# Scratch of q and k laid out by head and then feature, q and k loaded as 128 plain rows, and V's quarters in the order 0, 2, 1, 3, in a one-core decoder block

## The chip, the cores and the metric

The kernel runs on one core of a Trainium2 chip. Its engines are TensorE (PE in the profile, with its weight loads as PEld), VectorE (DVE), ScalarE (ACT), GpSimd (POOL) and SyncE (SP), which here does nothing but issue DMAs, in the order in which they stand in its queue. The data of all DMA queues is moved by 16 DMA engines. The metric is the device time of one execution in microseconds, as the median of several runs.

## The reference, cut to what matters

One layer of a decoder block on x of 2048 positions by 1024 features, all float32:

- `proj = x @ W_in + b_in`, with 9216 output columns: q, k and v for 3 groups of 8 heads of 64 features, two SiLU gates, the input of a gated linear recurrence, and two merge gates.
- Rotary embedding on q and k. Then dilated causal attention: group g has window and dilation (128, 1), (512, 4), (2048, 16). Queries and keys of one group are gathered by their residue modulo the dilation, and 128 queries attend to the keys of their own block of 128 and, in groups 0 and 1, of the block before.
- The three groups' outputs are combined per head slot, weighted by their softmax denominators, times a SiLU gate, and projected.
- A second branch: a causal convolution of width 4, the recurrence over positions, a SiLU gate, a projection.
- `out = (sigmoid(gA) * yA + sigmoid(gB) * yB) @ W_out + b_out`, and a layer norm of `alpha * x + out`.

## The kernel before, in words

Three stages follow one another on TensorE.

**Stage A, the projection (about 6 to 1437 us).** Features lie on the 128 partitions, positions in four chunks (c) of 512. Each pass of the plan takes two blocks of 128 output features through a Strassen-like scheme of products (line 639). Each factor is split in a high and a low part, so that three products stand for one in float32. q and k blocks hold two heads of 64 features: the weights' columns are permuted so that feature d of head h sits on partition 2d + h (`by_head`, line 274). After the rotation (`qk_chain`, line 320) a tile of 128 partitions by 512 positions (256 KB) is stored to a scratch in HBM, `qk_scr["q" or "k", u]`, one scratch of 128 rows by 2048 positions for each block u = 4g + hp of group g and head pair hp. q of group 2 and k of group 1 are stored grouped by residue (lines 350 and 353; runs of 32 and 128 positions), the others as plain rows of 512 positions (line 356). There are 96 such stores, 16 + 16 + 64.

**Stage B, attention (about 1437 to 1790 us).** It goes through 12 units u of one head pair of one group each (`unit(u)`: groups 0, 2, 1 for each head pair in turn), four steps G to a unit, 48 steps in all. Step G holds the scores of two blocks pairs (lines 994 and 1000, out of tile `qk`), their masking and exponential (DVE, ACT), the turning of the weights (line 1031), the values (line 1064, out of tile `V`), and, from G = 4 on, a half of a job of the other branch's projection (`yb`, line 1234). Tiles `qk` and `V` are double buffered by u % 2. q of unit u + 1 is loaded at the end of step 4u, k at 4u + 1 (`qk_parts`, line 794), V at 4u + 1 and 4u + 2 in four quarters of 32 partitions (`v_parts`, line 808). Since the scratch has the two heads in turn in its rows, q and k each are loaded in two halves: rows 0, 2, 4, ... to partitions 0 to 63, rows 1, 3, 5, ... to partitions 64 to 127 (line 803). Each half is 64 rows of 8 KB.

Every three units (one head pair done) the running maxima and sums go through HBM to be laid out anew: turned and stored (`ml_scr`, line 1088), loaded (`mt`, lines 1097, 1101, 1104), worked on in three steps by DVE, ACT and POOL (`weights`, line 1107), stored by POOL (`w_scr`, line 1145) and loaded as `wh` (line 1151). A matmul spreads them over the partitions (`w`, line 1158), and the three groups' outputs are weighted with them.

**Stage C (about 1790 us to the end)** holds what is left of `yb`, the attention branch's projection (`ya`) and the last product with the layer norm (`z`).

The order on every engine is the order in which the program's text runs. SP's queue carries nearly all loads and stores of stage B: q, k, V, `wlr` (weights of `yb`), `hx` (its input), `gB`, `yb_scr`, `ml_scr`, `mt`, `wh`, `ga`. The table `todo` (`at_group`) tells after which step an issue stands. In the built program each DMA that SP issues also waits until the one issued eight places before it has landed, since eight completion counters are used in turn.

Of the kernel before, what the change touches and what calls it, by code (L numbers as in the profile page):

```python
# [15 lines left out]
P = 128  # L16
# [4 lines left out]
CH = 512  # L21
# [10 lines left out]
def hybrid_block_kernel(ctx: ExitStack, tc: tile.TileContext, a: dict, out: bass.AP):  # L32
    nc = tc.nc
    sp, act, dve, pool, pe = nc.sync, nc.scalar, nc.vector, nc.gpsimd, nc.tensor

    def flat(t):
        return t.bitcast(F32)
# [14 lines left out]
    qk_scr = {(n, u): dram.tile([P, S], F32, name=f"{n}_scr{u}") for u in range(12) for n in ("q", "k")}  # L52
# [53 lines left out]
    def big(slot, shape, dt, name):  # L106
        return (cur["Z"] if slot[0] == "Z" else X).tile(shape, dt, name=name, tag=slot)
# [44 lines left out]
    def take(name, dt=F32R):  # L152
        if not vacant:
            raise RuntimeError(f"no slot at {now['n']}: {[x[1].name if hasattr(x[1],'name') else x[1] for x in home.values()]} chains {len(chains)}")
        i = vacant.pop(0 if now["n"] < now["last"] else vacant.index(min(vacant, key=LAST_SLOTS.index)))
        t = sl_p.tile([P, CH], dt, tag=f"s{i}", name=name)
        home[id(t)] = (i, t)
        return t

    def give(*ts):  # L160
        for t in ts:
            vacant.append(home.pop(id(t))[0])

    def give_sent(*ts):

        for t in ts:
            later(2, lambda t=t: give(t))
# [71 lines left out]
    def tt(eng, out, in0, in1, op):  # L239
        eng.tensor_tensor(out=out, in0=in0, in1=in1, op=op)  # L240
# [70 lines left out]
    lo_, up_ = slice(0, 64), slice(64, P)  # L311
# [4 lines left out]
    def blocks(t, g):  # L316

        return t.rearrange("p (r j) -> p j r", r=4 if g == 1 else 16)

    def qk_chain(rw, f, c):  # L320
        isq = f < FT_K
        u = f % 12
        g = u // 4
        nm = f"{f}_{c}"
        yield Ask(lag=0, need=1, ACT=1.3)
        sw = take("sw" + nm)
        scale = 0.125 if isq else 1.0
        act.activation(flat(sw)[lo_], flat(rw)[up_], AF.Copy, scale=scale)  # L328
        act.activation(flat(sw)[up_], flat(rw)[lo_], AF.Copy, scale=scale)  # L329
        yield Ask(lag=1, DVE=1.5 if c < 2 else 1.0, POOL=1.7)  # L330
        cos, sin = CS[c % 2]
        if isq:
            dve.scalar_tensor_tensor(out=flat(rw), in0=flat(rw), scalar=0.125, in1=cos, op0=ALU.mult, op1=ALU.mult)
        else:
            tt(dve, flat(rw), flat(rw), cos, ALU.mult)
        tt(pool, flat(sw), flat(sw), sin, ALU.mult)
        yield Ask(lag=1, need=1 if g else 0, DVE=(1.45 if c < 2 else 1.2) if g else 1.0)
        if g == 0:
            rp = rw
            tt(dve, flat(rp), flat(rw), flat(sw), ALU.add)  # L340
            give(sw)
        else:
            rp = take("rp" + nm)
            v, r = "p (j r) -> p j r", 4 if g == 1 else 16
            tt(dve, blocks(flat(rp), g), flat(rw).rearrange(v, r=r), flat(sw).rearrange(v, r=r), ALU.add)
            give(rw, sw)
        yield Ask()
        dst = qk_scr["q" if isq else "k", u]
        if isq and g == 2:
            sp.dma_start(dst.rearrange("p (r i) -> p r i", r=16)[:, :, 32 * c:32 * c + 32],  # L350
                         flat(rp).rearrange("p (r i) -> p r i", r=16))
        elif g == 1 and not isq:
            sp.dma_start(dst.rearrange("p (r i) -> p r i", r=4)[:, :, P * c:P * c + P],
                         flat(rp).rearrange("p (r i) -> p r i", r=4))
        else:
            sp.dma_start(dst[:, c * CH:(c + 1) * CH], flat(rp))
        give_sent(rp)


# [197 lines left out]
    qk = [("qk", FT_K + u, FT_Q + u) for u in range(12)]  # L557
# [26 lines left out]
    def result(s, fi, c, bank, u):  # L584
# [10 lines left out]
        if kind in ("qk", "v"):  # L595
            y = take("y" + nm)
            if kind == "v" and fi:
                dve.scalar_tensor_tensor(out=flat(y), in0=u, scalar=b72[:, f:f + 1], in1=bank, op0=ALU.add, op1=ALU.subtract)
            else:
                total(flat(y), bank, u, f, sgn, True)  # L600
            start_chain(qk_chain(y, f, c) if kind == "qk" else v_chain(y, f, c))
        elif kind == "mg":
            y = take("y" + nm, F32)
            total(y, bank, u, f, sgn, False)
            start_chain(mg_chain(y, sgn, f, c))
        elif kind == "ga" or not fi:
            y = take("y" + nm, F32)
            total(y, bank, u, f, sgn, False)
            start_chain(silu_chain(y, sgn, f, c))
        else:  # L610
            i = f - FT_U
            if c == 1 and i in put_off:
                y = take("y" + nm, F32)
                total(y, bank, u, f, sgn, True)
                act.activation(ubs[:, i, 2, 0:3], y[:, CH - 3:CH], AF.Copy)
                start_chain(store_chain(y, u_scr[i]))
                return
            ub = ub_free.pop(0)
            total(ub[:, 3:3 + CH], bank, u, f, sgn, True)
            start_chain(lru(i, c, ub), 7 if c % 2 else 0)  # L620
# [95 lines left out]
    for s, pl in enumerate(plan):  # L716
        if pl[0] and pl[4] == "ug":
            i = pl[1][1][0] - FT_U
# [68 lines left out]
    AT_X = {}  # L787
    UG = {0: 0, 2: 1, 1: 2}

    def unit(u):  # L790

        return (0, 2, 1)[u % 3], u // 3

    def qk_parts(u):

        g, hp = unit(u)

        def part(x, h, hs):
            def fn():
                if u < 2 and (x, h) == (0, 0):  # L800
                    AT_X["qk", u] = big(("X2", "X3")[u], [P, 2, S], F32, f"qk{u}")
                src = qk_scr["qk"[x], 4 * g + hp].rearrange("(d h) s -> h d s", h=2)
                sp.dma_start(AT_X["qk", u % 2][hs, x], src[h])
            return fn

        return [part(x, h, hs) for x in range(2) for h, hs in ((0, lo_), (1, up_))]

    def v_parts(u):
        g, hp = unit(u)
        src = v_scr[g][hp]  # L810

        def part(q):
            def fn():
                if u == 0 and q == 0:
                    AT_X["v"] = big("X4", [P, 2, 2, 16, 64], F32, "V")
                v = AT_X["v"][32 * q:32 * q + 32, u % 2]
                if g == 2:
                    sp.dma_start(v.rearrange("i s n x -> i (s n) x"), src[q].rearrange("s (a i) x -> i (s a) x", a=4))
                else:
                    for t in range(2):  # L820
                        sp.dma_start(v[:, t], src[t, q].rearrange("c (a i) x -> i (c a) x", a=4))
            return fn

        return [part(i) for i in range(4)]


    def biases():
# [45 lines left out]
    for t in sorted(early):  # L873
        for fn in early[t]:
            at(max(t, 0), fn)

    begin = {1: qk_parts(0), 3: v_parts(0), 5: qk_parts(1)}
    low = NS
    where = [(s, j) for s in range(NQ) for j in range(ticks[s])]
# [18 lines left out]
    n = len(where)  # L898
# [383 lines left out]
    def at_group(g, fn):  # L1282
        todo.setdefault(g, []).append(fn)
# [14 lines left out]
    for fn in v_parts(1):  # L1298
        at_group(1, fn)
# [6 lines left out]
        at_group((1, 1, 2, 2, 3, 3, 4, 4)[k], lambda k=k: split_h(k))  # L1306
    for u in range(1, 11):
        for i, fn in enumerate(qk_parts(u + 1)):
            at_group(4 * u + i // 2, fn)
        for i, fn in enumerate(v_parts(u + 1)):  # L1310
            at_group(4 * u + 1 + i // 2, fn)
    WS = {}
# [19 lines left out]
    for hp in range(3):  # L1332
        e = 4 * (3 * hp + 2) + 4
        for i in range(12):
            c, g = i // 3, (0, 2, 1)[i % 3]
# [3 lines left out]
    for G in range(NG + 1):  # L1339
# [30 lines left out]
        if y:  # L1370
            n, hf = divmod(halves[0], 2)
# [82 lines left out]
    for t in halves:  # L1454
        n, hf = divmod(t, 2)
# [139 lines left out]
    for t, tt in enumerate(TT):  # L1595
        c, b = divmod(t, 4)
# [67 lines left out]
```

## Time and profile before

| What | us |
|---|---|
| median of 3 runs (2122.76 to 2126.47) | 2124.85 |
| profiled execution, its time | 2128.92 |
| profiled execution, span from first to last instruction | 2127.1 |
| TensorE busy in the span | 2078.8 (98%) |
| VectorE, ScalarE, GpSimd busy | 1683.5, 1189.1, 763.6 |
| TensorE busy between 1420 and 1790 us | 343.57 of 370 |
| mean share of the 16 DMA engines between 1420 and 1790 us | 0.95 |

The profiled execution lies 4.07 us above the median of the runs; 1.8 us of its time lie outside the span. "DMA share" in a window is the busy time of the packets summed over the 16 engines, over 16 times the window; it can pass 1, since an engine may hold two packets at once. "PEclk" is the clock granted to TensorE as a share of the full one. The duration of an entry of SPq is the time that SP took to issue the DMAs, not the time of the transfer.

### The profile page before, as it was taken

The page shows a single profiled execution, that of the slowest core. Times are in us where ns is not written, and L with a number is a line of the kernel's source. Part 1 is how long each engine was busy: PE and PEld are TensorE (multiplying, and loading weights), DVE is VectorE, ACT ScalarE, POOL GpSimd, SP SyncE. Part 2 cuts the span into 40 slices and gives each one's busy share as a digit, 9 for nine tenths or more (in the row PEclk, how much of TensorE's full clock was granted, in tenths as well). Part 3 has the DMA queues.
Part 4 walks back from the last instruction along what each step waited for, and adds up shares of the span by engine and source line. Part 5 has one row for each costly group of instructions (what it writes and reads, how often), then busy time and mean ns, then how long its engine had stood idle before and what let it go on. Part 6 is the DMA issues. An engine that isn't in the chain of part 4 may idle for free. (4 is left out here: it accounts for less than half of the span.)

```text
span 2127.1 us, 35284 instructions
## 1 busy us (share of the span) xinstructions
PE 2078.8 (98%) x11877; PEld 1695.7 (80%) x11877; DVE 1683.5 (79%) x2985; ACT 1189.1 (56%) x2462; POOL 763.6 (36%) x685
## 2 busy tenths in 40 slices
PE   9999999999999999999999999998999889999998
PEld 7888888877788888888887888887877678778886
DVE  8788999988988868888887888756666567877667
ACT  6456455557467566677577777756666554321100
POOL 2544654553664200120120120116267478522120
PEclk9999999999999999999999999999999999999999
DMA  7877887976887866666665666679999996774431
GB/s 229 243 230 206 246 248 210 271 231 189 250 252 218 274 204 198 183 199 191 212 193 178 217 208 201 194 214 234 197 234 214 204 209 195 240 239 151 156 99 70
DMA packets 333445, 443.09 MB, mean 208 GB/s; under 512 B 164320, under 2 KB 174592, under 8 KB 330192
## 3 DMA queue, kind: packets, MB, share of 16 engines
q1 hardware_dynamic: 316624, 408.38, 65.0%
q0 software_dynamic: 11744, 23.54, 6.0%
q10 hardware_dynamic: 4896, 8.92, 1.1%
q8 instruction: 94, 1.54, 0.3%
q14 instruction: 87, 0.71, 0.1%
HBM read 289.74 MB, written 150.99 MB: 207 GB/s over the span
## 5 line engine op out<-in xcount | busy, mean ns | idle before, releaser
L639 PE MATMUL q<-xT,hS 128*128 128x512 f32 x1632 | 503.7, 390 | 0.0
L639 PE MATMUL q<-xT,l 128*128 128x512 f32 x1088 | 423.8, 390 | 3.0 <-DVE l L240 2.9
L639 PE MATMUL q<-xB,hA 128*128 128x512 f32 x1344 | 415.5, 390 | 0.3 <-ACT hA L284 0.3
L639 PE MATMUL q<-xB,l 128*128 128x512 f32 x944 | 367.2, 389 | 0.0
L639 PEld LDWEIGHTS q<-xT,hS 128*128 128x128 f32 x1632 | 305.5, 188 | 66.7 <-issue 3.3
L639 PEld LDWEIGHTS q<-xB,hA 128*128 128x128 f32 x1344 | 251.4, 188 | 56.8 <-issue 4.1
L639 PEld LDWEIGHTS q<-xT,l 128*128 128x128 f32 x1088 | 204.3, 188 | 47.5 <-DVE l L240 5.1
L240 POOL TENSOR_TENSOR sw<-sw,sin 128x512 f32<-128x512 f32 x96 | 155.4, 1624 | 157.9 <-ACT sw L329 85.9
L639 PEld LDWEIGHTS q<-xB,l 128*128 128x128 f32 x944 | 177.2, 188 | 36.8
L240 POOL TENSOR_TENSOR y<-y,h 128x512 f32<-128x512 f32 x28 | 39.1, 1398 | 385.3 <-DVE h L538 340.2
L1016 ACT ACTIVATE pb<-pb 128x192 f32<-128x192 f32 (+1 forms) x384 | 160.6, 421 | 30.1 <-DVE pb L1014 28.5
L639 PE MATMUL q<-xB,hS 128*128 128x512 f32 x544 | 167.7, 389 | 1.0 <-ACT hS L284 1.0
L639 PE MATMUL q<-xT,hA 128*128 128x512 f32 x544 | 168.0, 390 | 0.2 <-ACT hA L284 0.2
L284 ACT ACTIVATE hS<-S 128x512 fp32r<-128x512 f32 x170 | 108.3, 637 | 84.8 <-DVE S L240 69.6
L1234 PE MATMUL yb<-hx,wl 128*128 128x512 f32 x576 | 150.3, 402 | 1.9 <-POOL hx L1210 1.7
L284 ACT ACTIVATE hA<-wA 128x512 fp32r<-128x512 f32 x220 | 138.2, 635 | 21.1 <-DMA wA<-in_w_in_dram 5.5
L240 POOL TENSOR_TENSOR l<-wA,hA 128x512 fp32r<-128x512 f32 x68 | 107.7, 1584 | 77.3 <-ACT hA L284 45.5
L1234 PEld LDWEIGHTS yb<-hx,wl 128*128 128x128 f32 x576 | 104.9, 188 | 31.4 <-issue 6.8
L639 PEld LDWEIGHTS q<-xB,hS 128*128 128x128 f32 x544 | 102.0, 188 | 22.8 <-ACT hS L284 1.4
L639 PEld LDWEIGHTS q<-xT,hA 128*128 128x128 f32 x544 | 101.8, 188 | 22.6 <-issue 1.1
L328 ACT ACTIVATE sw<-y 64x512 f32<-64x512 f32 x96 | 60.6, 631 | 79.2 <-DVE y L580 71.8
L1510 POOL TENSOR_TENSOR me<-gA,me 128x512 f32<-128x512 f32 x30 | 47.7, 1604 | 159.3 <-DVE gA L1509 136.1
(215 smaller groups left out, 4340.1 us busy)
## 6 DMA issues: line engine op xcount, KB each, us to landing
wA<-in_w_in_dram SPq DMA_DIRECT2D x220, 256.0 KB
wl_scr<-l SPq DMA_DIRECT2D x102, 512.0 KB
l<-wl_scr SPq DMA_DIRECT2D x102, 512.0 KB
wS<-in_w_in_dram SPq DMA_DIRECT2D x102, 256.0 KB
wS<-in_w_in_dram POOLq DMA_DIRECT2D x68, 256.0 KB, 6.6
wlr<-in_w_f_dram SPq DMA_DIRECT2D x64, 256.0 KB
mg_scr<-y SPq DMA_DIRECT2D x59, 256.0 KB
v_scr<-vs SPq DMA_DIRECT2D x48, 256.0 KB
```

What stands on the lines that cost most here:

```text
L240: eng.tensor_tensor(out=out, in0=in0, in1=in1, op=op)
L284: act.activation(heads(h), heads(r, False), AF.Copy)
L328: act.activation(flat(sw)[lo_], flat(rw)[up_], AF.Copy, scale=scale)
L639: pe.matmul(bank, w[:, ks], x[:, kk, xx], start=(first and i == 0), stop=(last and i == 11))
L1016: act.activation(pp, pp, AF.Exp, scale=-1.0, bias=mm, accum_out=ll)
L1234: pe.matmul(YB["t"], w[:, a, k], hx(8 * c + k)[:, b], start=(hf == 0 and m == 0), stop=(hf == 1 and m == 11))
L1510: (dve if i in (6, 7) else pool).tensor_tensor(out=ME[c][:, f], in0=ga, in1=ME[c][:, f], op=ALU.add)
```

## The change

The scratch of q and k has the heads one after the other: row 64h + d instead of 2d + h. The tile in SBUF that is stored stays as it is (feature d of head h on partition 2d + h). So a plain store now writes each partition's row of 2 KB to row 64h + d, as one DMA whose HBM side has the shape 64 x 2 x 512. The two stores grouped by residue are each cut in two DMAs, one for a head, which read every second partition. A load of q or of k is then one DMA of 128 rows of 8 KB instead of two of 64 rows; part 0 (q) stays at step 4u, part 1 (k) at 4u + 1. V's quarters are loaded in the order 0, 2 (at 4u + 1), 1, 3 (at 4u + 2), instead of 0, 1 and 2, 3.

```diff
@@ qk_chain @@
         dst = qk_scr["q" if isq else "k", u]
-        if isq and g == 2:
-            sp.dma_start(dst.rearrange("p (r i) -> p r i", r=16)[:, :, 32 * c:32 * c + 32],
-                         flat(rp).rearrange("p (r i) -> p r i", r=16))
-        elif g == 1 and not isq:
-            sp.dma_start(dst.rearrange("p (r i) -> p r i", r=4)[:, :, P * c:P * c + P],
-                         flat(rp).rearrange("p (r i) -> p r i", r=4))
-        else:
-            sp.dma_start(dst[:, c * CH:(c + 1) * CH], flat(rp))
+        if g == 2 - (not isq):
+            r = 16 if isq else 4
+            n = CH // r
+            for h in range(2):
+                sp.dma_start(dst[64 * h:64 * h + 64].rearrange("d (r i) -> d r i", r=r)[:, :, n * c:n * c + n],
+                             flat(rp).rearrange("(d h) (r i) -> h d r i", h=2, r=r)[h])
+        else:
+            sp.dma_start(dst.rearrange("(h d) s -> d h s", h=2)[:, :, c * CH:(c + 1) * CH], flat(rp))
         give_sent(rp)
@@ qk_parts @@
-        def part(x, h, hs):
+        def part(x):
             def fn():
-                if u < 2 and (x, h) == (0, 0):
+                if u < 2 and x == 0:
                     AT_X["qk", u] = big(("X2", "X3")[u], [P, 2, S], F32, f"qk{u}")
-                src = qk_scr["qk"[x], 4 * g + hp].rearrange("(d h) s -> h d s", h=2)
-                sp.dma_start(AT_X["qk", u % 2][hs, x], src[h])
+                sp.dma_start(AT_X["qk", u % 2][:, x], qk_scr["qk"[x], 4 * g + hp])
             return fn
-        return [part(x, h, hs) for x in range(2) for h, hs in ((0, lo_), (1, up_))]
+        return [part(x) for x in range(2)]
@@ v_parts @@
-                if u == 0 and q == 0:
+                if u == 0 and not q:
...
-        return [part(i) for i in range(4)]
+        return [part(i) for i in (0, 2, 1, 3)]
@@ the table of steps @@
         for i, fn in enumerate(qk_parts(u + 1)):
-            at_group(4 * u + i // 2, fn)
+            at_group(4 * u + i, fn)
```

On SP, in stage A, around one of the stores grouped by residue. Before (`wl_scr` keeps low parts of weights, `rp` is a rotated tile, `wS` and `wA` are weights):

```order
L247 DMA wA_4_891<-in_w_in_dram 128x512
L350 DMA q_scr_106<-rp_1_865 2048x1x32
L301 DMA wl_scr_117<-l_3_835 128x1024
L356 DMA k_scr_107<-rp_0_918 128x512
L301 DMA wl_scr_117<-l_3_887 128x1024
L247 DMA wS_5_986<-in_w_in_dram 128x512
```

and of the change:

```order
L247 DMA wA_4_891<-in_w_in_dram 128x512
L353 DMA q_scr_106<-rp_1_865 1024x1x32 x2
L301 DMA wl_scr_117<-l_3_835 128x1024
L356 DMA k_scr_107<-rp_0_919 64x2x512
L301 DMA wl_scr_117<-l_3_887 128x1024
L247 DMA wS_5_987<-in_w_in_dram 128x512
```

One grouped store has become two in the same place, and the plain store has another shape; no other row of stage A stands elsewhere.

On SP, in stage B, from the load of q for unit 8 to the loads of `wh` for the second head pair. Before:

```order
L803 DMA qk_13619<-q_scr_102 64x2048 x2
L1218 DMA gB_16928<-mg_scr 128x512
L1245 DMA yb_scr<-gB_16680 128x512
L1088 DMA ml_scr_64<-mls_16926 64x128
L803 DMA qk_13619<-k_scr_103 64x2048 x2
L821 DMA V<-v_scr_84 32x16x64 x4
L1184 DMA wlr_17024<-in_w_f_dram 128x512
L821 DMA V<-v_scr_84 32x16x64 x4
L1151 DMA wh_13747<-w_scr_71 12x512
```

and of the change:

```order
L802 DMA qk_13651<-q_scr_102 128x2048
L1217 DMA gB_16943<-mg_scr 128x512
L1244 DMA yb_scr<-gB_16696 128x512
L1087 DMA ml_scr_64<-mls_16941 64x128
L802 DMA qk_13651<-k_scr_103 128x2048
L820 DMA V<-v_scr_84 32x16x64 x4
L1183 DMA wlr_17038<-in_w_f_dram 128x512
L820 DMA V<-v_scr_84 32x16x64 x4
L1150 DMA wh_13775<-w_scr_71 12x512
```

The q and k rows are one DMA each instead of two, in the same places; the eight V issues read alike, though the second two of the first four now go to partitions 64 to 95. TensorE, VectorE, ScalarE and GpSimd have the same instructions in the same order as before.

## The prediction

> **What bounds the kernel now.** I read first, in windows, whether TensorE stands anywhere, and how full the DMA engines are there (busy time of each engine, with its count of instructions, then TensorE's clock, DMA share and rate):
>
> ```profile
> core 0: us, PE busy (x) PEld busy (x) DVE busy (x) ACT busy (x) POOL busy (x), PEclk, DMA share, GB/s
> 1300.00:1420.00 120.00, 120.00 (x534) 97.82 (x533) 90.86 (x128) 88.67 (x138) 18.22 (x12) 1.00 0.65 206
> 1420.00:1790.00 370.00, 343.57 (x4231) 277.51 (x4230) 233.84 (x994) 224.56 (x911) 215.49 (x263) 0.98 0.95 212
> ```
>
> The end of stage A is TensorE alone: 120.00 busy of 120. Around stage B, TensorE stands 370 - 343.57 = 26.4 us, its clock is not full, and the DMA engines are 0.95 full while they move only 212 GB/s. So a change to stage B's transfers can win some 26 us and what the clock loses, no more. What TensorE waited for there:
>
> ```profile
> PE w L1158 <- DMA wh<-w_scr: 12.3, 3, 8.1
> PE pt L1031 <- ACT ptb L1044: 5.4, 3, 4.4
> PE pt L1031 <- ACT pb L1016: 2.2, 2, 2.1
> PE yb L1234 <- POOL hx L1210: 1.7, 3, 0.7
> ```
>
> Never for q, k or V themselves, which are loaded a unit ahead. It waits for `wh`, a load of 24 KB. TensorE's order of time at its four longest stops (start, duration, last the idle time before it):
>
> ```profile
> 1568.43 0.47 PE L1158 MATMUL w<-wh,sel 128*128 128x512 f32 x1 [1.54 <-DMA wh<-w_scr]
> ...
> 1662.88 0.76 PE L1158 MATMUL w<-wh,sel 128*128 128x512 f32 x1 [8.09 <-DMA wh<-w_scr]
> ...
> 1729.38 0.72 PE L1031 MATMUL pt<-ident,pb 64*128 64x64 f32 x16 [4.36 <-ACT ptb L1044]
> ...
> 1755.06 0.47 PE L1158 MATMUL w<-wh,sel 128*128 128x512 f32 x1 [2.62 <-DMA wh<-w_scr]
> ```
>
> Why `wh` is late stands in SP's order of time ahead of the longest stop, beside what the same issues take when nothing holds them (minimum/median/maximum in ns), and the median from issue to landing of `w_scr`, from which `wh` is loaded:
>
> ```profile
> 1633.75 0.88 SPq L1184 DMA_DIRECT2D wlr<-in_w_f_dram  x2
> 1634.73 1.14 SPq L803 DMA_DIRECT2D qk<-q_scr  x2
> 1635.92 0.58 SPq L1218 DMA_DIRECT2D gB<-mg_scr  x1
> 1639.00 0.33 SPq L1245 DMA_DIRECT2D yb_scr<-gB  x1
> 1639.43 0.47 SPq L1088 DMA_DIRECT2D ml_scr<-mls  x1
> 1639.95 1.23 SPq L803 DMA_DIRECT2D qk<-k_scr  x2
> 1642.47 5.55 SPq L821 DMA_DIRECT2D V<-v_scr  x4
> 1648.19 4.71 SPq L1184 DMA_DIRECT2D wlr<-in_w_f_dram  x2
> 1652.95 2.58 SPq L821 DMA_DIRECT2D V<-v_scr  x4
> 1656.01 4.23 SPq L1151 DMA_DIRECT2D wh<-w_scr  x4
> ```
>
> ```profile
> L821 SPq DMA_DIRECT2D V<-v_scr x64: 303/488/3979, 1427.1 to 1748.6; - x64
> L1151 SPq DMA_DIRECT2D wh<-w_scr x16: 333/362/3007, 1563.1 to 1824.2; - x16
> ```
>
> ```profile
> w_scr<-whl POOLq DMA_DIRECT2D x8, 48.0 KB, 7.3
> ```
>
> Four V issues take 5.55 us instead of 4 x 0.488 = 1.95, two `wlr` 4.71 instead of 0.88, four V 2.58, four `wh` 4.23 instead of 4 x 0.362 = 1.45. Together SP loses 3.60 + 3.83 + 0.63 + 2.78 = 10.8 us between 1642 and 1660, held by transfers that are not through. The 8.09 us stop is this backlog, and the first transfers in it are q's and k's halves.
>
> **The rate of those halves.** Three windows in which one kind of transfer prevails: loads of weights and x over 128 rows at the start, q and k of unit 0 in halves, V's quarters.
>
> ```profile
> 10.00:20.00 10.00, 10.00 (x45) 8.27 (x45) 9.34 (x18) 9.71 (x18) 0.00 (x0) 1.00 1.04 386
> 1427.00:1433.00 6.00, 6.00 (x28) 4.99 (x27) 1.82 (x3) 0.63 (x1) 0.00 (x0) 1.00 1.01 215
> 1633.00:1635.00 2.00, 2.00 (x44) 1.93 (x40) 1.48 (x9) 2.00 (x10) 1.79 (x4) 1.00 1.39 159
> ```
>
> At an equally full DMA (1.04 and 1.01), loads over 128 partitions bring 386 GB/s, those over 64 bring 215. Row length can't be the cause: the halves have the longer rows (8 KB against 2 KB). So I take it that a transfer over half of the partitions has about half of the way into SBUF.
>
> **The change part by part.**
>
> *q and k as one DMA of 128 rows.* A unit's q and k are 2 x 128 x 8 KB = 2.10 MB: 9.75 us at 215 GB/s, 5.43 at 386. The new load itself is in no row. Lower bound of its worth: 0, if the rate stays; upper: 4.3 us a unit, 52 us of queue time over twelve units, which brings the share from 0.95 to about 0.95 - 52/370 = 0.81. I take the upper, since the nearest row is of the same partitions. SP also issues 24 DMAs fewer.
>
> Longest stop: if only 4.3 us of the 10.8 go, `wh` comes 4.3 earlier and 8.09 - 4.3 = 3.8 remain. But SP stands until 1639.00 for `yb_scr` whatever the DMA does; q (2.7 us at the new rate) is then through, and k, issued at 1639.95, is through by about 1643, just as V's issue begins at 1642.47. So V and `wlr` find free engines, and the whole 10.8 us can go. Next late is `w_scr`, which POOL issues here:
>
> ```profile
> 1642.74 1.09 POOL L1145 DMA_DIRECT2D w_scr<-whl  x2 [0.30 <-POOL whl L240]
> ```
>
> Its end at 1643.83 and 7.3 to landing give 1651.1; 1.45 for the `wh` issues and the 2.64 that lie today between their end (1660.24) and TensorE's start give 1655.2, against 1654.79 when TensorE stops. Residue 0.4; gain **7.7 us** (between 4.3 and 8.09).
>
> The two shorter `wh` stops, 1.54 and 2.62, are below 4.3 and have the same issues ahead: gain **4.2 us** (between 0 and 4.2).
>
> The clock around the long stop:
>
> ```profile
> 1656.00:1663.00 7.00, 0.12 (x1) 0.15 (x1) 0.00 (x0) 0.00 (x0) 3.68 (x4) 0.66 0.85 103
> 1663.00:1667.00 4.00, 4.00 (x28) 3.16 (x30) 1.47 (x5) 0.41 (x2) 0.00 (x0) 0.50 0.81 224
> 1667.00:1671.00 4.00, 4.00 (x36) 3.40 (x35) 2.49 (x15) 3.70 (x18) 0.00 (x0) 0.81 1.03 223
> 1730.00:1735.00 5.00, 5.00 (x42) 4.52 (x39) 2.81 (x11) 2.88 (x14) 1.01 (x2) 0.66 1.07 282
> 1740.00:1790.00 50.00, 47.38 (x569) 38.26 (x568) 34.05 (x133) 30.31 (x125) 36.44 (x38) 1.00 0.70 175
> ```
>
> After 8.09 us of standing, TensorE works at 0.50 and 0.81: 4 x 0.50 + 4 x 0.19 = 2.8 us lost. After 4.36 us it loses 5 x 0.34 = 1.7; after 2.62 us (within 1740 to 1790) nothing. Gain with the long stop gone: **2.8 us**.
>
> The 4.36 us stop is ACT standing 6.42 us for `mt`, whose preparation stands on POOL behind splits of `hx`; POOL itself waited for a DMA only here:
>
> ```profile
> 1711.63 0.62 POOL L1209 CAST hx<-hx 128x512 fp32r<-128x512 f32 x1 [1.11 <-DMA hx<-hb_scr]
> 1728.33 0.52 ACT L1131 ACTIVATE mt<-mt 32x384 f32<-32x384 f32 x1 [6.42 <-DMA V<-v_scr]
> ```
>
> So an earlier DMA gives 1.1 at most of it; I take **0.9** (between 0 and 4.36 + 1.7).
>
> *V's quarters 0, 2, 1, 3.* Quarters 0 and 1 in a row run at 159 GB/s, so a unit's 1.05 MB take 6.6 us. If 0 and 2 ran side by side, each on its own half, it would be 3.3: worth 0 to 3.3 us of queue time a unit. No row shows two quarters of different halves in flight. I take 0, since they stand one after the other in one queue; and more would change little, the stops it could shorten being counted as gone. [...]
>
> *The stores.* Stage A gets 32 more DMAs. The grouped stores' issues:
>
> ```profile
> L350 SPq DMA_DIRECT2D q_scr<-rp x16: 519/564/967, 69.6 to 1271.0; - x16
> L353 SPq DMA_DIRECT2D k_scr<-rp x16: 518/542/577, 462.1 to 1407.7; - x16
> ```
>
> Each half of such a store takes between half of that and all, so SP has 32 x 0.28 to 0.56, 9 to 18 us, more in 1340. The 64 plain stores (64 x 2 x 512) might fall to the lower rate: 262 KB take 0.68 us at 386 and 1.22 at 215, so 64 x 0.54 = 35 us more of queue time. The cover is the DMA share of 0.65 and TensorE's 120.00 of 120: weights come ahead of time. I take 0; without the cover, up to 18 + 35 = 53 us.
>
> **Sum:** 7.7 + 4.2 + 2.8 + 0.9 = 15.6 us, against the profiled execution 2128.92 - 15.6 = 2113.3. That execution lies 4.07 us above the median of the runs. If none of the 4.07 lies in these stops, the median falls to 2124.85 - 15.6 = 2109.3; if all does, to 2113.3. I take the middle: **2111 us**.
>
> **Rivals.**
>
> *Half of the long stop stays.* V's slow quarters hold SP even without q and k, or POOL's chain to `w_scr` becomes the last. For it: V moves but 159 GB/s and stands nearest ahead of `wh`; `w_scr` has a margin of only 0.4 us. Against: SP's pause until 1639.00. Then 4.3 of the long stop and 4.2 of the short ones go, the clock still falls (3.8 lies nearer to 4.36, where it fell, than to 2.62): 8.5 us, 2116. [...]
>
> *The change doesn't do what it says: the rate stays at 215.* For it: no row has 8 KB rows over 128 partitions, and 212 GB/s is what the whole stage moves. Against: 386 in the first row at the same share. Then nothing goes: 2125.
>
> *Slower: the stores hold back stage A.* Place: SP's queue, where weights (`wA`, `wS`, `l`) stand behind the stores; price up to the 53 us above, less 15.6: 2162. It decides once each of the 96 stores costs TensorE over (15.6 + 4.2)/96 = 0.21 us. Against it: TensorE never waits for a DMA in the row of 1300 to 1420.
>
> **How the numbers follow.** Forecast 0.60, half stays 0.18, rate stays 0.14, slower 0.08. Low end: all of the waits quoted for TensorE (21.6) and both clock losses (4.5) but what ACT's own chain keeps, some 4: 2124.85 - 22, about 2103. High end: 2122, past the second case; what lies above is the two last, 0.22 together. 0.2% (4.2 us) is about what a measurement of this kernel tells from no change. Faster by more: 0.78; within: 0.14; slower: 0.08.
>
> **What would show it.** Right: in stage B a DMA share of some 0.8, q and k of unit 0 at over 330 GB/s, V and `wlr` issues near their medians at the second head pair, no stop of `w` for `wh` over 1 us, the clock at 1.00 from 1650 to 1670. Wrong: a share near 0.95 (rate stays); `w` still waiting over 3 us with SP held at V or at `w_scr` (half stays); new idle time at line 639 (stores).

## The result, and the profile after

The changed kernel takes 2104.37 us in the median (2102.49 to 2105.95, 4 runs), the kernel before beside it 2125.66 (4 runs). The ratio is **0.9893, 95% interval 0.9862 to 0.9923**: 22.7 us less (16.4 to 29.3). Forecast were 2111 us, a gain of 15.6 us by the sum and 13.9 in the stated time. The profiled execution took 2103.79 us against 2128.92, 25.1 us less; its span is 2102.0.

The same windows as before, of the kernel after. Stage B now ends about 26 us earlier, so the second row ends at 1770 (columns as in the prediction's windows):

```profile
core 0: us, PE busy (x) PEld busy (x) DVE busy (x) ACT busy (x) POOL busy (x), PEclk, DMA share, GB/s
1300.00:1420.00 120.00, 120.00 (x535) 97.86 (x534) 90.38 (x128) 89.15 (x139) 18.24 (x12) 1.00 0.65 206
1420.00:1770.00 350.00, 344.13 (x4261) 279.58 (x4260) 238.01 (x1000) 226.20 (x914) 220.79 (x267) 1.00 0.84 229
1427.00:1431.00 4.00, 4.00 (x19) 3.31 (x18) 1.07 (x2) 0.61 (x1) 0.55 (x1) 1.00 0.97 373
1650.00:1670.00 20.00, 20.00 (x248) 15.77 (x247) 15.70 (x55) 13.27 (x55) 12.00 (x11) 1.00 0.94 251
```

TensorE stands 350 - 344.13 = 5.87 us around stage B, where it stood 26.4. q and k of unit 0 as 128 rows come at 373 GB/s where the halves came at 215. The DMA share fell from 0.95 to 0.84, and the clock from 1650 to 1670 us is 1.00, where it was 0.50 to 0.81 behind the long stop. The waits of TensorE in stage B (1420 to 1770 us), all that the view lists:

```profile
PE pt L1030 <- ACT pb L1015: 2.2, 2, 2.1
PE pt L1030 <- ACT ptb L1043: 1.3, 2, 0.9
PE o L1063 <- issue: 0.8, 1, 0.8
PE mlt L1084 <- DVE o L1079: 0.6, 1, 0.6
PE w L1157 <- DMA wh<-w_scr: 0.5, 1, 0.5
```

And the four places of the longest stops before, in TensorE's order of time:

```profile
1564.21 0.39 PE L1157 MATMUL w<-wh,sel 128*128 128x512 f32 x1
...
1646.34 0.47 PE L1157 MATMUL w<-wh,sel 128*128 128x512 f32 x1
...
1706.80 0.72 PE L1030 MATMUL pt<-ident,pb 64*128 64x64 f32 x16 [0.94 <-ACT ptb L1043]
...
1728.74 0.47 PE L1157 MATMUL w<-wh,sel 128*128 128x512 f32 x1 [0.50 <-DMA wh<-w_scr]
```

The starts lie 4.2, 16.5, 22.6 and 26.3 us ahead of those before. Beside the waits that the prediction showed, the same view of the kernel before lists these:

```profile
PE o L1064 <- issue: 1.4, 1, 1.4
PE s L994 <- issue: 1.3, 1, 1.3
PE pt L1031 <- DVE ptb L1046: 1.2, 1, 1.2
PE mlt L1085 <- DVE o L1080: 0.5, 1, 0.5
```

So the 25.1 us between the two profiled executions can be read off row by row:

| Term | before | after | gain, us | forecast, us |
|---|---|---|---|---|
| `w` for `wh` | 12.3 | 0.5 | 11.8 | 11.9 |
| `pt` for `ptb` | 5.4 | 1.3 | 4.1 | 0.9 |
| `yb` for `hx` | 1.7 | 0 | 1.7 | 0 |
| small waits (rows above, `pb`) | 6.6 | 3.6 | 3.0 | 0 |
| clock after the long stop | 2.8 | 0 | 2.8 | 2.8 |
| clock after the 4.36 us stop | 1.7 | 0 | 1.7 | 0 |
| sum | | | 25.1 | 15.6 |

The waits for `wh` and the clock after the long stop came as forecast. What was missed are the four other rows, 9.5 us together. (The lead of 26.3 us at the last `w` shrinks to 25.1 by the end of the kernel, so the table closes to about 1 us, not to the tenth. Single rows vary more: a second execution of the changed kernel, further down, waits 3.1 us for `ptb` where this one waits 1.3.) SP's order of time at the second head pair, after:

```profile
1630.53 0.32 SPq L1244 DMA_DIRECT2D yb_scr<-gB  x1
1630.94 0.50 SPq L1087 DMA_DIRECT2D ml_scr<-mls  x1
1631.50 0.58 SPq L802 DMA_DIRECT2D qk<-k_scr  x1
1632.32 2.06 SPq L820 DMA_DIRECT2D V<-v_scr  x4
1634.49 3.09 SPq L1183 DMA_DIRECT2D wlr<-in_w_f_dram  x2
1637.63 2.25 SPq L820 DMA_DIRECT2D V<-v_scr  x4
1640.42 3.53 SPq L1150 DMA_DIRECT2D wh<-w_scr  x4
```

V's first four issues take 2.06 us instead of 5.55, and `wh` is issued 12.45 us after the issue of k began (1643.95 - 1631.50), where that took 20.29 (1660.24 - 1639.95). SP is still held for some 4.7 us, by the medians that the prediction used, 4.3 of them in the two `wlr` (3.09 against 0.88) and in `wh` (3.53 against 1.45). The backlog shrank; it is not gone. What holds SP inside an issue stands in no row. For the first `wh` it is not the completion counter: the DMA issued eight places before it had landed at 1639.70 us (the trace also records when each DMA lands), ahead of the 1640.42 at which that issue began.

### The profile page after: what moved, and what is told of

It reads as the page before. It is cut to its first block, busy times and chain, and to the rows that moved or that the text cites. A ratio compares the mean times of both kernels' runs of the same rounds, so it can differ in the third digit from the quotient of the medians.

```text
span 2102.0 us, 35297 instructions
## 1 busy us (share of the span) xinstructions
PE 2074.7 (99%) x11877; PEld 1694.6 (81%) x11877; DVE 1679.4 (80%) x2985; ACT 1189.4 (57%) x2462; POOL 765.3 (36%) x685
## 3 DMA queue, kind: packets, MB, share of 16 engines
q8 instruction: 94, 1.54, 0.3%
## 4 chain that ended last, share of the span: by engine, by line
PE 64%; DVE 4%; DMA 4%; issue 3%; ACT 3%; POOL 2%; SPq 1%; DVEq 0%; POOLq 0%; ACTq 0%
PE q L639 39%; PE yb L1233 5%; PE o L1063 3%; PE z L1540 3%; PE z L1539 3%; PE z L1538 3%; PE pt L1030 2%; PE s L999 2%; PE ya L1506 1%; PE ya L1507 1%; PE ya L1505 1%; PE g L497 1%; PE s L993 1%; DMA atr<-at_scr 1%; SPq L1103 0%
```

## The experiments

The theory: a load over partitions 0 to 63 or 64 to 127 has half the way (215 GB/s for q's and k's halves, 373 for the whole loads), so q, k and V fill the queue and hold SP; whole loads end that. Its rivals were that the new scratch, not the load's partitions, brings the gain; that V's order does; and that the ACT stop went for a reason of its own. Every kernel was compared with runs of the kernel before on the same chip. Differences in us are the ratio's, times the median of those runs.

### V's order alone, q and k alone, and the new scratch without whole loads

Three kernels part the change. The first is the kernel before with V's new order and nothing else:

```diff
-        return [part(i) for i in range(4)]
+        return [part(i) for i in (0, 2, 1, 3)]
```

> The kernel before with V's quarters in the order 0, 2, 1, 3 and nothing else. Theory (backlog of q's and k's half loads): the stops of TensorE for wh stay (12.3 us before), the time is 0 to 3 us below the kernel before. Rival (the gain comes from V's order): at least half of the changed kernel's 21 us, so 10 us or more below, and the 8.09 us stop gone.

The second is the changed kernel with V's old order:

```diff
-        return [part(i) for i in (0, 2, 1, 3)]
+        return [part(i) for i in range(4)]
```

> The changed kernel with V's quarters back in the order 0, 1, 2, 3. Theory: 19 to 22 us below the kernel before, no stop for wh over 1 us, ACT's stop for mt gone. Rival (V's order): 11 us or less below, stops for wh of some 5 us in all.

The third has the changed kernel's scratch, its stores and V's new order, but loads q and k in halves again, each half now 64 plain rows. It differs from the first by the scratch and the stores alone:

```diff
-                sp.dma_start(AT_X["qk", u % 2][:, x], qk_scr["qk"[x], 4 * g + hp])
+                for hs in (lo_, up_):
+                    sp.dma_start(AT_X["qk", u % 2][hs, x], qk_scr["qk"[x], 4 * g + hp][hs])
```

> The changed kernel, its stores and V's order as they are, but q and k loaded in two DMAs again: rows 0 to 63 to partitions 0 to 63, rows 64 to 127 to partitions 64 to 127. Theory (what counts is that one DMA reaches both halves of the partitions): as slow as V's order alone, 0 to 3 us below the kernel before, about 215 GB/s in unit 0's loads, stops for wh of 10 us or more. Rival (rows one after the other in HBM instead of every second one, or the stores' new layout, bring the gain): 10 us or more below the kernel before.

| Kernel | median, us | ratio | 95% interval | difference, us |
|---|---|---|---|---|
| V's order alone | 2119.90 | 0.9972 | 0.9959 to 0.9986 | -6.0 |
| q and k alone | 2108.95 | 0.9912 | 0.9892 to 0.9932 | -18.7 |
| halves of plain rows, V's new order | 2123.43 | 0.9982 | 0.9967 to 0.9996 | -3.8 |

Windows in stage B, first of q and k alone, then of the halves of plain rows:

```profile
1427.00:1431.00 4.00, 4.00 (x19) 3.30 (x19) 0.69 (x1) 0.41 (x1) 0.55 (x1) 1.00 1.00 403
1420.00:1790.00 370.00, 362.23 (x4338) 293.36 (x4337) 248.37 (x1012) 231.73 (x924) 233.62 (x281) 1.00 0.86 229
```

```profile
1427.00:1431.00 4.00, 4.00 (x20) 3.30 (x19) 0.69 (x1) 0.31 (x2) 0.55 (x1) 1.00 1.02 211
1420.00:1790.00 370.00, 350.47 (x4257) 283.26 (x4257) 238.97 (x999) 226.51 (x914) 219.79 (x266) 0.98 0.93 217
```

Halves bring 211 GB/s, of plain rows too, and whole loads 403, so the rate of these loads hangs on their partitions and not on the rows in HBM. Most of the gain stands with q's and k's whole loads: 18.7 us, a little short of the 19 expected. With them TensorE waits only 0.6 us for `wh` in all, and ACT's stop shrinks to 1.69 us, though it is not gone. The new scratch by itself brings no gain: the halves of plain rows are not faster than V's order alone (-3.8 against -6.0 us; the intervals overlap). Their waits:

```profile
PE pt L1031 <- ACT ptb L1044: 6.4, 2, 6.2
PE w L1158 <- DMA wh<-w_scr: 6.1, 3, 3.4
```

They sum to 12.5 us, instead of 17.7 before and 17.1 with V's order alone, and the long one has moved from `wh` to `ptb`. Expected were at least 10 us for `wh` alone; that missed. With the backlog there, which stop becomes the long one seems to depend on a few us; that was not tested.

V's order alone gains 6.0 us, between the two expectations, and the interval excludes 0. The stops for `wh` stay, as the theory had it: 10.0 us in all, 6.4 of them at the long one. The prediction's 0 for V's order is wrong.

### Which half it is

To tell "half of the partitions" from "64 rows are too few", unit 0's q and k came first to partitions 32 to 95 (64 rows, 1.05 MB), then to 0 to 31 and 96 to 127:

```diff
-                sp.dma_start(AT_X["qk", u % 2][:, x], qk_scr["qk"[x], 4 * g + hp])
+                if u:
+                    sp.dma_start(AT_X["qk", u % 2][:, x], qk_scr["qk"[x], 4 * g + hp])
+                    return
+                for hs in ((slice(0, 32), slice(96, P)) if x else (slice(32, 96),)):
+                    for y in range(2):
+                        sp.dma_start(AT_X["qk", 0][hs, y], qk_scr["qk"[y], 4 * g + hp][hs])
```

> The changed kernel, but unit 0's q and k come in six DMAs: first q and k for partitions 32 to 95 (64 rows each, both halves of the partitions), then q and k for 0 to 31, then for 96 to 127 (32 rows each, one half). Theory (half of the partitions, half of the way): the first 1.05 MB at 300 GB/s or more, the other 1.05 MB at about 215. Rival (64 rows in a DMA are too few, whichever they are): both parts at about 215. The time of the kernel stays within 3 us of the changed kernel under both, since unit 0's loads are hidden behind stage A.

Its windows:

```profile
1424.00:1427.00 3.00, 3.00 (x15) 2.49 (x14) 0.69 (x1) 0.72 (x1) 0.52 (x1) 1.00 0.95 330
1427.00:1431.00 4.00, 4.00 (x19) 3.33 (x18) 1.38 (x2) 0.63 (x1) 0.03 (x1) 1.00 1.03 234
```

64 rows in the middle come at 330 GB/s, and what then goes to the outer quarters at 234, with the DMA engines about as full in both. So neither the count of rows nor their length makes these loads slow: 64 rows to partitions that straddle the middle came at 330 GB/s, where 64 rows to one half came at 211. The one execution took 2104.53 us; unit 0's loads are far from any stop.

### Bringing one stop back

If the backlog of halves makes the stops, then the halves of one unit should bring back one stop. First of unit 8, whose loads stand ahead of `wh` of the second head pair:

```diff
-                sp.dma_start(AT_X["qk", u % 2][:, x], qk_scr["qk"[x], 4 * g + hp])
+                for hs in (lo_, up_) if u == 8 else (slice(0, P),):
+                    sp.dma_start(AT_X["qk", u % 2][hs, x], qk_scr["qk"[x], 4 * g + hp][hs])
```

> The changed kernel, but unit 8's q and k alone are loaded in halves of plain rows again (the loads ahead of the longest stop). Theory (each stop comes from the backlog of the unit just ahead of it): w waits 3 to 8 us for wh at the second head pair and nowhere else over 1 us; the time is 4 to 11 us above the changed kernel's 2104, so 2108 to 2115. Rival (the backlog adds up over many units, one does little): less than 2 us above, w waits under 2 us.

TensorE at the second head pair:

```profile
1650.73 0.47 PE L1158 MATMUL w<-wh,sel 128*128 128x512 f32 x1 [3.10 <-DMA wh<-w_scr]
```

The stop is back with 3.10 us, where the changed kernel has none, and all other waits for `wh` make 0.4 us. The median is 2108.84 (ratio 0.9907, 0.9891 to 0.9923). By the ratio that is 3 us above the changed kernel, a little under what was expected, and the intervals overlap: the stop is shown, its price in time is not.

Then of unit 9, with `u == 9` in the same lines:

> The changed kernel, but unit 9's q and k alone are loaded in halves of plain rows (the loads ahead of the four loads of hx on which POOL waited 2.4 and 1.1 us before ACT's 4.36 us stop). Theory (ACT's stop came from hx being issued and landing late): the stop of pt for ACT at the third head pair is back at 2 to 4.4 us, POOL waits for hx 2 us or more in all, 2 to 6 us above the changed kernel. Rival (ACT's stop came from the long stop one head pair earlier, which shifted POOL's work): no stop over 1 us, within 1 us of the changed kernel.

POOL and TensorE around the ACT stop, with unit 9 in halves:

```profile
1686.13 0.60 POOL L1209 CAST hx<-hx 128x512 fp32r<-128x512 f32 x1 [1.64 <-DMA hx<-hb_scr]
...
1712.79 0.92 PE L1031 MATMUL pt<-ident,pb 64*128 64x64 f32 x16 [2.67 <-ACT ptb L1044]
```

Here `w` hardly waits for `wh` (0.8 us at most), and the ACT stop comes back to 2.67 us behind a late `hx`. With unit 8 in halves it is the other way round: the long stop is there, POOL does not wait for `hx`, and the ACT stop is 0.92 us. So the ACT stop comes with a late `hx`, which is the DMA queue's doing, and not from a shift that the long stop had brought. The wait for `hx` is a little under the 2 us expected. Median 2109.68, ratio 0.9910 (0.9892 to 0.9929), 3.5 us above the changed kernel, with intervals that overlap. The size alone would prove little, since a second execution of q and k alone has 2.36 us without any halves; the table below carries the reading.

The prediction had this wrong through one row of the kernel before, which it did not quote:

```profile
1701.56 0.60 POOL L1209 CAST hx<-hx 128x512 fp32r<-128x512 f32 x1 [2.37 <-PE w L1158]
```

Read as the profile names it, POOL waits for TensorE. But this is the same work, on another tile, as the row at 1711.63 that waits 1.11 us for the DMA; a wait is put down to the event that came last by the profile, and TensorE's `w` ended at 1701.54, just ahead of POOL's start. The landing records decide it: the load of this tile landed at 1701.43 us, 0.13 us before POOL starts, and the load for the row at 1711.63 landed at 1711.51, 0.12 us before. Two more waits of the table are put down to TensorE (1.56 and 1.42), and there too the load landed 0.13 us before POOL starts. So all of them are waits for `hx`; in the kernel before they make 3.48 us, and one sum holds in every execution:

| Execution | POOL's waits for `hx`, us | stop of `pt`, us | difference, us |
|---|---|---|---|
| before | 2.37 + 1.11 | 4.36 | 0.88 |
| V's order alone | 1.04 + 2.66 | 4.67 | 0.97 |
| V in the order 0, 3, 1, 2 | 0.60 + 2.41 | 4.10 | 1.09 |
| V in the order 0, 1, 3, 2 | 1.82 + 1.97 | 4.62 | 0.83 |
| halves of plain rows | 1.56 + 3.41 | 6.16 | 1.19 |
| unit 9 in halves | 1.64 | 2.67 | 1.03 |
| q and k alone | 0.77 | 1.69 | 0.92 |
| q and k alone, again | 1.42 | 2.36 | 0.94 |
| changed, again | 0.83 | 1.70 | 0.87 |
| changed | 0 | 0.94 | 0.94 |
| unit 8 in halves | 0 | 0.92 | 0.92 |
| unit 0 in middle and outer parts | 0 | 0.92 | 0.92 |
| V's pieces in turn | 0 | 0.92 | 0.92 |

The stop is about 1 us plus all that POOL waits for `hx`. The chain's own part is that 1 us, and not the 3.5 that the prediction left standing (4.36 - 0.9).

### What in V's order does it

Two more orders, in the kernel before. In 0, 3, 1, 2 neighbours again lie in different halves; in 0, 1, 3, 2 they lie in the same half, as in 0, 1, 2, 3:

```diff
-        return [part(i) for i in range(4)]
+        return [part(i) for i in (0, 3, 1, 2)]
```

> The kernel before with V's quarters in the order 0, 3, 1, 2: both pairs still hold one quarter of each half of the partitions. Theory (quarters of both halves in turn use more of the way into SBUF): as V's order alone, ratio 0.996 to 0.999 of the kernel before, V's loads shorter than before. Rival (0, 2, 1, 3 is special, or its gain was chance): no difference from the kernel before.

> The kernel before with V's quarters in the order 0, 1, 3, 2: each pair holds two quarters of the same half. Theory: no gain, ratio 0.999 to 1.001, V's loads as long as before. Rival (any other order than the one before, or chance): ratio below 0.998, as V's order alone.

| V's order, q and k in halves | median, us | ratio | 95% interval | DMA share in stage B | mean of a V load of 128 KB, issue to landing, us |
|---|---|---|---|---|---|
| 0, 2, 1, 3 | 2119.90 | 0.9972 | 0.9959 to 0.9986 | 0.93 | 7.37 |
| 0, 3, 1, 2 | 2120.88 | 0.9962 | 0.9948 to 0.9976 | 0.92 | 7.01 |
| 0, 1, 3, 2 | 2126.43 | 0.9990 | 0.9974 to 1.0006 | 0.95 | 7.63 |

The rows of the DMA share, of 0, 2, 1, 3, of 0, 3, 1, 2 and of 0, 1, 3, 2:

```profile
1420.00:1790.00 370.00, 347.21 (x4255) 280.89 (x4253) 238.04 (x998) 225.93 (x915) 220.76 (x267) 0.98 0.93 217
```

```profile
1420.00:1790.00 370.00, 354.56 (x4286) 286.12 (x4286) 241.76 (x1004) 228.66 (x918) 226.49 (x273) 0.99 0.92 220
```

```profile
1420.00:1790.00 370.00, 348.27 (x4249) 281.12 (x4248) 238.44 (x999) 226.26 (x914) 218.71 (x266) 0.98 0.95 215
```

Both orders that change the half gain, and the one that doesn't shows no gain that can be told from 0. In each of the first two the DMA engines are less full (0.93 and 0.92, against 0.95 before). (Part of the fall comes from the window, which holds more of stage C when the kernel is faster. From 1420 to 1770 us, within stage B in all four, the shares are 0.98 before, 0.95, 0.94 and 0.97.) V's loads are shorter too in the first two, by the landing records of 56 loads from 1460 to 1770 us: the kernel before has a mean of 7.60 us, and two executions of one kernel agree to 0.1 us (6.27 and 6.37 in the changed one). What makes them shorter is not shown. Being in flight together is not enough: in the kernel before, where neighbours lie in the same half, a piece of V issued at 1644.47 us counts its first completion at 1651.62, before the piece ahead of it has landed (1653.20). That neighbours in different halves get in each other's way less is the likeliest reading; it was not shown.

### The changed kernel again, without V's order, and with V's pieces in turn

Measured together, on one chip: the changed kernel, q and k alone, and the changed kernel with V's 128 KB pieces of groups 0 and 1 issued in turn for the two halves (quarter 0, 2, 0, 2, then 1, 3, 1, 3) instead of two of a quarter in a row:

```diff
-        def part(q):
+        def part(j, t):
...
-                if g == 2:
-                    sp.dma_start(v.rearrange("i s n x -> i (s n) x"), src[q].rearrange("s (a i) x -> i (s a) x", a=4))
-                else:
-                    for t in range(2):
+                for q in (j + 2 * t,) if g == 2 else (j, j + 2):
+                    v = AT_X["v"][32 * q:32 * q + 32, u % 2]
+                    if g == 2:
+                        sp.dma_start(v.rearrange("i s n x -> i (s n) x"), src[q].rearrange("s (a i) x -> i (s a) x", a=4))
+                    else:
...
-        return [part(i) for i in (0, 2, 1, 3)]
+        return [part(j, t) for j in range(2) for t in range(2)]
```

> The changed kernel as it is, once more, beside the two below on one chip. Theory: ratio to the kernel before 0.987 to 0.992, so that V's order on top of q and k is worth its difference to the next run.

> The changed kernel with V's quarters in the order 0, 1, 2, 3, once more. Theory (V's order shortens the same backlog as q and k, so it gives less on top than alone): 1 to 4 us above the changed kernel. Rival (the two gains add up): 6 us above.

> The changed kernel, and in groups 0 and 1 the pieces of 128 KB alternate between the halves one by one (quarter 0 piece 0, quarter 2 piece 0, quarter 0 piece 1, quarter 2 piece 1, then the same for 1 and 3). Theory: V's loads a little shorter, but stage B's standing is down to 6 us of which V can hold at most 1 to 2, so within 2 us of the changed kernel. Rival (V still holds TensorE): 3 us or more below it.

| Kernel | median, us | ratio | 95% interval |
|---|---|---|---|
| changed, again | 2105.90 | 0.9893 | 0.9873 to 0.9914 |
| q and k alone, again | 2110.14 | 0.9910 | 0.9889 to 0.9931 |
| V's pieces in turn | 2101.53 | 0.9875 | 0.9852 to 0.9897 |

The first two repeat their ratios (0.9893 and 0.9912). In both pairs V's order brings some 4 us on top of q and k (22.7 - 18.7, and 2110.14 - 2105.90), at the upper edge of the 1 to 4 expected and under the rival's 6. The intervals of a pair overlap; that both say the same is what stands for it.

V's pieces in turn have the lowest median of all, 4.4 us under the changed kernel beside them, more than the 2 us expected; here too the intervals overlap. Stage B of the changed kernel again, then with the pieces in turn:

```profile
1420.00:1770.00 350.00, 342.29 (x4257) 277.82 (x4256) 238.94 (x999) 225.97 (x914) 219.68 (x266) 1.00 0.84 229
```

```profile
1420.00:1770.00 350.00, 343.05 (x4255) 278.04 (x4254) 237.56 (x999) 226.29 (x914) 219.98 (x266) 1.00 0.81 228
```

The share falls once more, by 0.03, and V's loads of 128 KB take 5.90 us from issue to landing, against 6.37 in the changed kernel beside them. But TensorE stands only 0.8 us less there, and the profiled executions lie 1.8 us apart (2103.10 and 2101.29). Where the rest of the 4.4 us lies, or whether it is there, stays open.

## Why the prediction was wrong, and what it had right

The forecast gain was 15.6 us by the sum, 13.9 in the stated time; 22.7 went. From 2124.85, where the prediction started, the measured ratio gives 2102.1 us, a little below its low end of about 2103. The mechanism was right (whole loads of q and k relieve the queue, and the stops for `wh` go). Three terms failed: the ACT stop, the waits that were not costed, and V's order. The low end failed with them: it counted only the waits that were quoted, and left ACT's own chain 4 us where that chain keeps about 1.

**The rate of the halves: right.** 373 GB/s at a share of 0.97 where 386 was taken; the bound of 0 for the worth of the whole load is out. The share in stage B came down to 0.84, not quite to 0.81, with 1.00 of the clock.

**The long stop: right in size, the way to it only in part.** 8.09 us went, 7.7 were forecast. But the step "V and `wlr` find free engines, and the whole 10.8 us can go" failed by 4.7: V nearly did, `wlr` and `wh` still lost 2.2 and 2.1. Nor is `w_scr` what comes last:

```profile
1633.90 1.09 POOL L1144 DMA_DIRECT2D w_scr<-whl  x2 [0.30 <-POOL whl L240]
```

It was issued by 1634.99 us and had landed by 1640.37 (5.4 us, not the 7.3 that were reckoned). SP waited 0.5 us for it and then stood in the issues of `wh` until 1643.95; with the 2.64 us that followed before, that gives 1646.6, and TensorE came to `w` at 1646.34. The stop is gone with nothing to spare, and SP's queue is still its likeliest limit. Unit 8 in halves, which brought 3.10 us back, shows how thin the margin is.

**The two short stops and the clock after the long one: right.** 1.54 and 2.62 became 0 and 0.50, and the clock is 1.00 from 1650 to 1670. The rival "half of the long stop stays" falls, and "the rate stays at 215" too. That a stop of 2.62 us costs no clock was read from one row, and it is no rule: in the runs above the granted clock was 0.51 to 0.60 over the 3 to 4 us behind stops of 1.92, 1.97, 2.67 and 3.10 us (V's order alone, halves of plain rows, unit 9, unit 8), and 0.55 from 1444 to 1447 us in the kernel before, behind a stop of 2.05 us that ended at 1441.57; it was 1.00 behind stops of 2.36 us (q and k alone, again) and 2.62 us. The length of the stop alone does not decide it there.

**The stores: right that they are hidden, wrong in their price.** The issues after:

```profile
L353 SPq DMA_DIRECT2D q_scr<-rp x32: 512/662/979, 70.0 to 1272.4; - x32
L353 SPq DMA_DIRECT2D k_scr<-rp x32: 518/571/1322, 463.0 to 1409.3; - x32
L356 SPq DMA_DIRECT2D q_scr<-rp x16: 542/548/578, 453.6 to 1406.7; - x16
```

Half of a grouped store takes 0.66 or 0.57 us, as much as the whole took (0.56 and 0.54) or more, where half of that to all was reckoned. A plain store takes 0.55 us where the same one took 0.32:

```profile
L356 SPq DMA_DIRECT2D q_scr<-rp x16: 319/320/382, 452.7 to 1405.9; - x16
```

The other plain stores stand at 0.33 before and 0.52 to 0.55 after. So SP spends about 32 x 0.66 + 32 x 0.57 - 32 x 0.55 + 64 x 0.22 = 36 us more in stage A, and not 9 to 18. TensorE's 120.00 of 120 at the end of stage A did not move, and over the first 1420 us it was busy 1410.0 us, 1409.2 before: the issues cost twice the most that was reckoned, and the slower rival still didn't come.

**The 4.36 us stop: the step that failed most.** "POOL itself waited for a DMA only here", so "an earlier DMA gives 1.1 at most of it; I take 0.9". It gave 3.4 of the 4.36 (and 4.1 over all `ptb` waits), and with the stop under 1 us the clock's 1.7 came too: 5.8 in place of 0.9. (In the second execution of the changed kernel the stop is 1.70, so 2.7 went.) As the table shows, POOL had waited 3.48 us for `hx`, not 1.1, and the stop follows those waits one for one. The error was to believe a named releaser whose time fitted, where the same instruction 10 us later was named with the DMA.

**Waits that were not costed.** `yb` for `hx` and the rows under 1.5 us, 4.7 us in all, were left at 0. The prediction's opening had bounded them ("some 26 us and what the clock loses"); the sum then took up the four longest stops alone.

**V's order taken as 0: wrong.** It is worth 6.0 us alone and some 4 on top of q and k. The reason given, "they stand one after the other in one queue", does not keep two of them from being in flight together, and "the stops it could shorten being counted as gone" was true only for the four that had been counted. Nor was 159 GB/s the rate of quarters 0 and 1: the two V loads in flight from 1633 to 1635 us are those of line 818 issued from 1630.39, quarters 2 and 3 of a unit of group 2, with a load of `gB` behind them. The share fell by 0.03 or 0.04 of the 350 us up to 1770, where the order that gains nothing fell by 0.01: as an estimate 7 to 11 us of queue time over twelve units, 0.6 to 0.9 a unit. The prediction's own range, 0 to 3.3 us a unit, holds that; what was wrong was to take its 0. With SP held in line, queue time can stand on TensorE's path at many places; which of them V's order shortened was not traced.

**From the profile to the median.** Half of the 4.07 us was taken off. The profiled executions differ by 25.1 us, the medians by 22.7 (by the ratio), so some 2 us of discount was right; with intervals of several us that may be luck. The miss, 8.8 us of the stated gain, fits the 9.5 us that the sum left out.

## What to carry to other kernels

When the DMA queue is the cause, count every wait of the stage that stands behind that queue, the small ones and those on other engines with another name, and not only the stops that name the DMA; the bound at the top (standing time plus clock) was here nearer to the truth than the sum of its four largest rows. Before a named releaser is believed, look at the same instruction one round earlier or later, and at when the DMA that it could have waited for landed. A load's partitions can matter more than its rows (here 64 rows came at 211 GB/s to one half and at 330 to the middle): look at the rate of each kind of transfer at equal DMA share, and let neighbours in a queue lie in different halves where they can't be whole (worth 6.0 us here for V's quarters alone).

## What the runs showed of the hardware that was not expected

- 64 partitions in the middle (32 to 95) load at 330 GB/s (one execution), 0 to 63 or 64 to 127 at 211 to 219, whole loads at 343 to 403 (seven executions, 1427 to 1431 us). So the 64 in the middle pass the rate of a half without spanning all 128 partitions; why they do is not shown.
- With V's quarters of different halves behind one another in the queue the DMA share between 1420 and 1770 us was 0.95 and 0.94, where it was 0.98 before, and with the pieces in turn 0.81 instead of 0.84; the new order with neighbours of the same half left 0.97.
- What SP took to issue a store went by its shape and not by its bytes: 0.32 us for 128 rows of 2 KB, 0.55 for the same bytes with the scratch's two heads apart, 0.57 to 0.66 for one half of a grouped store whose whole took 0.54 to 0.56.
- The granted clock was 0.51 to 0.60 behind stops of TensorE as short as 1.92, 1.97 and 2.05 us, and 1.00 behind others of 2.36 and 2.62 us.
